# HGRN's transposes and its level of 64 tokens put into the runs of its level products, and HGRN's steps with products held back to follow RWKV's, in a hybrid decoder layer

## The chip, the cores and the metric

The program runs on one core of a Trainium2 chip. The metric is the device time of one execution in microseconds (us). Every comparison is of such times of this kernel before and after the change, on the same inputs.

## What is computed

One decoder layer over 2048 tokens of width 1024, all in float32. An input projection `h @ W_in` feeds two token mixers that run side by side: HGRN2 (4 heads of 128) and RWKV-7 (8 heads of 64). Their outputs are concatenated, projected and added to `x`; a ConvFFN with a depthwise convolution of width 3 follows, and a final RMSNorm. Cut to what matters here:

```
proj = rmsnorm(x, norm1_w) @ w_in
o_hg = HGRN2: S_t = diag(f_t) S_{t-1} + k_t v_t^T,  o_t = S_t^T q_t,  k = 1 - f
o_rw = RWKV-7: S_t = S_{t-1} diag(w_t) + (S_{t-1} a_t) b_t^T + v_t k_t^T,  y_t = S_t r_t
x = x + concat(o_hg, o_rw) @ w_out
x = x + (silu(gate) * val) @ w_down,   gate, val = split(conv3(rmsnorm(x, norm2_w) @ w_up))
out = rmsnorm(x, final_norm_w)
```

## The kernel before

**Two stages.** Stage 1 (`phase1`) does the input projection, both mixers and the output projection of the first three blocks of 512 tokens; stage 2 does the last block's output projection (`wacc`, line 1270) and the ConvFFN. The change touches stage 1 alone.

**Dense products.** A large product is three matmuls of 128 rows by 512 columns, because each operand is split into a high and a low part of type float32r (`mm3`, lines 270 to 272; the weights' split is on lines 254 and 255). Their accumulator in stage 1 is the tile `pj`. They use the whole 128 x 128 array of TensorE (the PE of the profile).

**Small products.** The mixers work with plain float32 products, most of them on a part of the array. In the names of the profile: `rw<-XH,M` and `rw<-AR,XH` (lines 905, 910) are RWKV's eight chunk steps, on 64 x 64 parts; `rw<-TZ,M`, `rw<-TTs,ZT` and `rw<-RHS,TTs` (lines 821, 834, 847) are three links of RWKV's triangular inverse, each of which waits for ScalarE (ACT) to copy the one before out of PSUM (tiles `ZT`, `TTs`, then `UV` and `M`); `rw<-UV,KBT` (line 867) waits for the last of these copies. `hg<-hX` are HGRN's level products: levels of 1 to 16 tokens on line 990 and of 32 tokens on line 997, on 32 columns of the array, and the level of 64 tokens on line 1046, on 64 columns. Whole-array products of HGRN are its transposes (`hg<-ident,hv` line 952, `hg<-ident,hk` line 1044), its state products (`hg<-VT,KT` line 1055) and its output products (`hg<-Af,VT`, `hg<-hq,SH`, lines 1064 and 1065). Sums over a head are float32r products over the whole array (`part,ones` for HGRN, `part,group` for RWKV, in `add_up`, lines 1083 and 1084).

**Order of work.** Three generators are advanced in rounds: RWKV (`rw_stream`, 8 calls of `rw_super`, each for two pairs of heads and 512 tokens), HGRN (`hg_stream`, 16 calls of `hg_unit`, each for one head and 512 tokens) and `dense`. A round is one step of RWKV (up to its next `yield`), one step of HGRN, and then dense work of about 2000 units of cost (`TICK`), which is three groups of three dense matmuls:

```
while any(alive.values()):
    for key, g in (("r", rw_), ("h", hg_)):
        if alive[key]:
            try:
                next(g)
            except StopIteration:
                alive[key] = False
    fill(TICK)
```

The scheduling layer then orders the instructions of each engine from this record, by data, buffers and its own estimates; on the chip each engine runs its list in that order.

**A unit of HGRN** has 15 steps: transpose of `v`; three steps that scale operands on VectorE (DVE) for the levels of 1, 2 and 4 tokens; the products of the diagonal and these levels; three more scalings; the products of the levels of 8, 16 and 32 tokens, which ACT copies into `Af` in six pieces; the scaling of level 64 and of `k` and `q`; the transpose of `k` with the products of level 64, copied by ACT to `KT` and `Af`; the state products; the output products and their square; the sum over the head; the last scaling and the store.

**PSUM.** HGRN has two banks (`bank("hg")`), RWKV two double banks, dense two. A unit takes eight `hg` banks in turn. `hX` has three buffers; the tile `KT` takes the buffer of `Sf`.

Of the kernel before, what the change touches and what calls it, by code (L numbers as in the profile page):

```python
# [18 lines left out]
P = 128  # L19
# [3 lines left out]
BLK = 512  # L23
# [44 lines left out]
def tile_layer(ctx, tc, consts, x, norm1_w, w_in, hg_lb_logits, hg_norm_w, rw_shift_mu, rw_w0, rw_w2,  # L68
# [205 lines left out]
    def phase1(c1):  # L274
# [371 lines left out]

        def rw_super(nb, s_):
# [20 lines left out]
            for u in U:  # L668
                TE.matmul(bs_[u][:, 0, :], w2a2[64:128, pc[u]], tl[64:128, :], start=True, stop=True)
                TE.matmul(bs_[u][:, 1, :], w2a2[0:64, pc[u]], tl[0:64, :], start=True, stop=True)  # L670
# [52 lines left out]
            for j in range(2):  # L723
                for u in U:
                    s1 = bank2()
                    for i in range(4):
                        b, e = 2 * j + i // 2, i % 2
                        for h in range(2):
                            hr = slice(h * 64, h * 64 + 64)
                            TE.matmul(s1[:, h, i * P:i * P + P], KB[hr, 4 * u + b, 2 * e:2 * e + 2, :],  # L730
                                      AR[hr, u, :, 2 * b + e, :], start=True, stop=True)
# [31 lines left out]
            for u in U:  # L763
                for b in range(4):
                    TE.transpose(tp[:, u, b * P:(b + 1) * P], AT[:, u, 2 * b:2 * b + 2, :], ident)
            tpv = tp.rearrange("p u (b h t) -> p (u b) h t", h=2, t=64)
            tq = bank2()
            for u in U:
                for b in range(4):
                    TE.matmul(tq[:, u, b * P:(b + 1) * P], v[:, u, b * P:(b + 1) * P], cen, start=True, stop=True)  # L770
# [9 lines left out]
            for b, h, e, u in quads():  # L780
                kr, c0, sl = 64 - er0(e), col0(u, e), (b * 2 + h) * 64
                TE.matmul(lv[c0:c0 + 64, u, sl:sl + 64], M[kr:kr + 64, e, u, b, h, 0:64],
                          UV[kr:kr + 64, 4 * u + b, e, h * 64:h * 64 + 64], start=True, stop=True,
                          tile_position=(kr, c0))
            lvv = lv.rearrange("p u (b h t) -> p u b h t", h=2, t=64)
# [32 lines left out]
            for b, h, e, u in quads():  # L818
                r0 = er0(e)
                c0, sl = r0 + 32 - 32 * u, u * 256 + (b * 2 + h) * 32  # L820
                TE.matmul(z[c0:c0 + 32, 0, sl:sl + 32], M[r0:r0 + 32, e, u, b, h, 32:64],
# [9 lines left out]
            for b, h, e, u in quads():  # L831
                r0 = er0(e)
                c0, sl = r0 + 32 * u, u * 256 + (b * 2 + h) * 32
                TE.matmul(z2[c0:c0 + 32, 0, sl:sl + 32], ZT[r0 + 32:r0 + 64, u * 8 + b * 2 + h, :],
# [10 lines left out]
            for b, h, e, u in quads():  # L845
                r0, c0, sl = er0(e), col0(u, e), ((b % 2) * 2 + h) * P
                TE.matmul(qus[u][c0:c0 + 64, b // 2, sl:sl + P], TTs[r0:r0 + 64, u * 8 + b * 2 + h, :],
# [15 lines left out]
            for u in U:  # L863
                for ch in range(8):
                    b, e = ch // 2, ch % 2
                    for h in range(2):
                        TE.matmul(xp[h * 64:h * 64 + 64, u, ch * 64:ch * 64 + 64], KBT[:, u, ch, h * 64:h * 64 + 64],
                                  UV[:, 4 * u + b, e, h * 64:h * 64 + 64], start=ch == 0, stop=False,
                                  tile_position=(0, h * 64), skip_group_check=True)
            for u in U:  # L870
                Q, G = M[:, 0, u, :, :, 0:64], M[:, 1, u, :, :, 0:64]
                yg = bank2()
                for w in range(2):
                    for b in range(4):
                        for e in range(2):
                            rs_ = slice(er0(e), er0(e) + 64)
                            sl = w * 256 + b * 64
                            for h in range(2):
                                rhs = (M[rs_, e, u, b, h, 64:128] if w == 0
                                       else KBT[rs_, u, 2 * b + e, h * 64:h * 64 + 64])  # L880
                                TE.matmul(yg[h * 64:h * 64 + 64, e, sl:sl + 64], Q[rs_, b, h, :], rhs,
# [8 lines left out]
            for u in U:  # L890
                for ch in range(8):
                    b, e = ch // 2, ch % 2
                    for h in range(2):
                        c0 = (h ^ u) * 64
                        TE.matmul(yp[c0:c0 + 64, u, ch * 64:ch * 64 + 64],
# [3 lines left out]
            for ch in range(8):  # L899
                b, e = ch // 2, ch % 2  # L900
                cs_ = slice(ch * 64, ch * 64 + 64)
                for u in U:
                    for h in range(2):
                        hr = slice(h * 64, h * 64 + 64)
                        TE.matmul(xp[hr, u, cs_], M[hr, 1, u, b, e, 0:64], XH[hr, u, ch, :], start=False,
                                  stop=ch == 7, tile_position=(h * 64, h * 64), skip_group_check=True)
                for u in U:
                    for h in range(2):
                        hr, c0 = slice(h * 64, h * 64 + 64), (h ^ u) * 64
                        TE.matmul(yp[c0:c0 + 64, u, cs_], XH[hr, u, ch, :], RT[hr, u, ch, :], start=False,  # L910
# [714 lines left out]
```

## Time and profile before

| | us |
|---|---|
| median of 3 runs | 2649.24 |
| lowest and highest run | 2648.57 and 2652.3 |
| the profiled execution | 2645.42 |
| its span, first to last instruction | 2643.6 |
| TensorE busy in that span | 2547.0 |
| VectorE busy | 1963.7 |
| ScalarE busy | 1372.7 |
| GpSimd busy | 382.1 |

All rows of the trace come from the profiled execution, so a row's time is counted from the start of its span. In a row of the timeline the first number is the start and the second the time until the last of the merged instructions ends; consecutive matmuls overlap, so what a matmul costs is read from the starts of its neighbours. A float32 product appears as two matmuls in the trace (x8 there is x4 in the program). `[0.72 <-DVE TZ L808]` says that the engine stood idle for 0.72 us before the row, until that instruction was done.

### The profile page before, as it was taken

The numbers are of one execution on the slowest core, as the hardware profiler recorded it, in microseconds if no ns is written. First come the engines' busy times: TensorE is split into PE (matmuls) and PEld (weight loads), VectorE is DVE, ScalarE is ACT, GpSimd is POOL, SyncE is SP. The second block draws the span as 40 slices with busy tenths as digits, with TensorE's granted clock in tenths as the row PEclk, the third lists the DMA queues.
The fourth block names the chain that finished last, engine by engine and source line by source line (L and its number), as shares of the span: only waits on it lengthen the run. The fifth ranks groups of instructions, "written<-read, shape, count | busy, mean of one in ns | idle before, by whom it ended". The sixth has DMA issues, their size and how long they took to land.

```text
span 2643.6 us, 51054 instructions
## 1 busy us (share of the span) xinstructions
PE 2547.0 (96%) x19467; PEld 2046.8 (77%) x19467; DVE 1963.7 (74%) x3744; ACT 1372.7 (52%) x2258; POOL 382.1 (14%) x686
## 2 busy tenths in 40 slices
PE   7999999999999999899899999999999999999998
PEld 5877777777777767777678888887888887888887
DVE  4868677676576765777678789988988887766556
ACT  5555444555545555344466654556554544545444
POOL 6433222212222122232100000000000000000000
PEclk9999999999999999999999999999999999999999
DMA  8846463555655565845583467747763553998655
GB/s 304 239 147 195 152 168 116 143 159 205 190 173 138 174 212 179 261 151 150 181 287 124 136 221 257 240 154 232 245 203 129 171 171 128 334 321 283 200 191 187
DMA packets 380298, 518.98 MB, mean 196 GB/s; under 512 B 114463, under 2 KB 211093, under 8 KB 380053
## 3 DMA queue, kind: packets, MB, share of 16 engines
q1 hardware_dynamic: 325521, 337.38, 40.1%
q0 software_dynamic: 54464, 178.32, 20.9%
q8 instruction: 153, 2.51, 0.4%
q14 instruction: 92, 0.75, 0.1%
q10 hardware_dynamic: 68, 0.02, 0.0%
HBM read 372.99 MB, written 134.22 MB: 192 GB/s over the span
## 4 chain that ended last, share of the span: by engine, by line
PE 70%; DVE 11%; ACT 8%; DMA 7%; issue 3%; POOL 0%; SPq 0%; DVEq 0%; ACTq 0%; POOLq 0%
PE pj L270 7%; PE pj L271 7%; PE pj L272 6%; PE ua L270 5%; PE ua L272 5%; PE ua L271 5%; PE da L271 3%; PE da L272 3%; PE da L270 3%; PE ud L271 2%; PE ud L270 2%; PE ud L272 2%; PE db L272 2%; PE db L271 2%; PE db L270 2%
## 5 line engine op out<-in xcount | busy, mean ns | idle before, releaser
L270 PE MATMUL pj<-hh,wh 128*128 128x512 f32 x960 | 391.6, 408 | 6.1 <-ACT rkv L122 4.0
L271 PE MATMUL pj<-hl,wh 128*128 128x512 f32 x960 | 377.4, 393 | 0.0
L272 PE MATMUL pj<-hh,wl 128*128 128x512 f32 x960 | 377.4, 393 | 0.0
L270 PE MATMUL ua<-Bh,uwh 128*128 128x512 f32 x704 | 276.4, 393 | 3.5 <-ACT m L122 2.2
L272 PE MATMUL ua<-Bh,uwl 128*128 128x512 f32 x704 | 274.3, 390 | 0.0
L271 PE MATMUL ua<-Bl,uwh 128*128 128x512 f32 x704 | 274.1, 389 | 0.0
L270 PEld LDWEIGHTS pj<-hh,wh 128*128 128x128 f32 x960 | 180.9, 189 | 54.5 <-issue 7.0
L272 PEld LDWEIGHTS pj<-hh,wl 128*128 128x128 f32 x960 | 180.8, 188 | 39.4 <-DMA wl<-Win171l 0.3
L271 PEld LDWEIGHTS pj<-hl,wh 128*128 128x128 f32 x960 | 181.0, 189 | 35.0 <-DVE hl L488 0.5
L254 ACT CAST uwh<-uraw 128x512 fp32r<-128x512 f32 x220 | 134.3, 617 | 135.0 <-PE ua L271 55.7
L255 DVE TENSOR_TENSOR dal<-draw,dah 128x512 fp32r<-128x512 f32 x138 | 95.2, 690 | 108.3 <-ACT dah L254 105.7
L255 DVE TENSOR_TENSOR uwl<-uraw,uwh 128x512 fp32r<-128x512 f32 x220 | 147.1, 684 | 34.3 <-ACT uwh L254 34.3
L254 ACT CAST dah<-draw 128x512 fp32r<-128x512 f32 x138 | 85.8, 621 | 160.0 <-PE da L271 75.5
L270 PEld LDWEIGHTS ua<-Bh,uwh 128*128 128x128 f32 x704 | 132.2, 188 | 33.9 <-ACT m L122 5.6
L272 PEld LDWEIGHTS ua<-Bh,uwl 128*128 128x128 f32 x704 | 132.2, 188 | 28.1 <-DVE uwl L255 0.4
L271 PEld LDWEIGHTS ua<-Bl,uwh 128*128 128x128 f32 x704 | 132.3, 188 | 26.7
L270 PE MATMUL ud<-Bh,uwh 128*128 128x512 f32 x352 | 138.0, 392 | 0.0
L1495 POOL DMA_DIRECT2D gd<-y x2 | 1.1, 542 | 943.1 <-DVE y L1493 943.1
L272 PE MATMUL ud<-Bh,uwl 128*128 128x512 f32 x352 | 137.1, 390 | 0.0
L271 PE MATMUL ud<-Bl,uwh 128*128 128x512 f32 x352 | 137.0, 389 | 0.0
L271 PE MATMUL da<-dbl,dah 128*128 128x512 f32 x332 | 129.4, 390 | 0.2 <-DVE dbl L255 0.2
L272 PE MATMUL da<-dbh,dal 128*128 128x512 f32 x332 | 129.2, 389 | 0.0
(582 smaller groups left out, 6203.0 us busy)
## 6 DMA issues: line engine op xcount, KB each, us to landing
uraw<-in_w_up_dram SPq DMA_DIRECT2D x176, 256.0 KB, 3.2
woraw<-in_w_out_dram POOLq DMA_DIRECT2D x96, 256.0 KB, 3.6
br<-gd SPq DMA_DIRECT2D x88, 256.0 KB, 4.3
draw<-Sg SPq DMA_DIRECT2D x88, 256.0 KB, 3.0
draw<-Tw SPq DMA_DIRECT2D x88, 256.0 KB, 3.9
gd<-y SPq DMA_DIRECT2D x86, 256.0 KB, 3.0
Sg<-br SPq DMA_DIRECT2D x72, 256.0 KB, 2.2
xt<-x1d SPq DMA_DIRECT2D x32, 512.0 KB, 6.5
```

The lines of the kernel that those rows point to most:

```text
L254: S.copy(hi, src)
L255: V.tensor_sub(lo, src, hi.bitcast(F32))
L270: TE.matmul(acc, lh, rh, start=first, stop=False, skip_group_check=skip)
L271: TE.matmul(acc, lh, rl, start=False, stop=False, skip_group_check=skip)
L272: TE.matmul(acc, ll, rh, start=False, stop=last, skip_group_check=skip)
L1495: (dma if end is None else nc.gpsimd.dma_start)(gd_[2 * h + b][fb * P:(fb + 1) * P, :], ys[0][:, b * BLK:(b + 1) * BLK])
```

## The change

`small` wraps every product of the two mixers. It notes the last product of RWKV's step; when a step of HGRN has been chosen to follow it, the first product of that step is given an ordering on TensorE behind it (no wait between engines). A step of HGRN that is marked `"products"` by the `yield` ahead of it is held back for up to two rounds until RWKV's step of the same round issues products; the other steps go as before. In `hg_unit` the transposes of `v` move behind the first level products, level 64 and the transposes of `k` move into the step with the levels of 8 to 32, and level 64 takes the last quarter pair of the bank `l1` (columns 256 to 511) and the buffer `SH` for its operand. A unit then has 13 steps, five of them marked, and takes seven banks. As the rounds are recorded, 80 marked steps occur: 63 of them follow a step of RWKV with products, 16 go alone after two rounds of waiting, and one goes alone because RWKV is over; 52 rounds have no step of HGRN. The number of rounds (386) stays, and so does every instruction, but for ScalarE's table loads: 53 in the order before and 59 after, in the whole program.

```diff
+        turn_ = {"now": None, "r": None, "h": None}
+        def small(f, *args, **kw):
+            i_ = f(*args, **kw)
+            if turn_["now"] == "r":
+                turn_["r"] = i_
+            elif turn_["h"] is not None:
+                tc.add_manual_dep(i_.ins, turn_["h"].ins.name, NOSYNC, reason="one run")
+                turn_["h"] = None
+            return i_
...
-            VT = rp.tile([P, 4, P], F32, tag="VT", name="VT")
-            tp = bank("hg")
-            for b in range(4):
-                TE.transpose(tp[:, b * P:(b + 1) * P], v[:, b * P:(b + 1) * P], ident)
-            act(VT, tp.rearrange("p (b t) -> p b t", t=P), AF.Copy)
-            yield
...
+            def turned(tag, name, src):
+                t_ = rp.tile([P, 4, P], F32, tag=tag, name=name)
+                tp = bank("hg")
+                for b in range(4):
+                    small(TE.transpose, tp[:, b * P:(b + 1) * P], src[:, b * P:(b + 1) * P], ident)
+                act(t_, tp.rearrange("p (b t) -> p b t", t=P), AF.Copy)
+                return t_
...
                 Xs.append(scaled(l))
-                yield
+                yield "products" if l == 2 else None
             l1 = bank("hg")
             level(l1, 192, k, q)
             for l in range(3):
                 level(l1, l * 64, Xs[l], Xs[l], l)
+            VT = turned("VT", "VT", v)
...
+            X = scaled(6)
+            V.tensor_mul(k, k, Sf)
+            V.tensor_mul(q, q, Pf)
+            yield "products"
             l1 = bank("hg")
             for l in range(3, 5):
                 level(l1, (l - 3) * 64, Xs[l - 3], Xs[l - 3], l)
             across(l1, 128, Xs[2])
+            for b in range(4):
+                small(TE.matmul, l1[0:64, 256 + b * 64:320 + b * 64], X[:, b * P:b * P + 64], X[:, b * P + 64:b * P + 128],
+                          start=True, stop=True, tile_position=(0, 0))
+            KT = turned("Sf", "KT", k)
...
+        nxt, held = None, 0
         while any(alive.values()):
+            turn_["r"] = None
+            step("r", rw_)
+            if nxt == "products" and (held < 0 or turn_["r"] is None and alive["r"] and held < 2):
+                held += 1
+            else:
+                turn_["h"] = turn_["r"] if nxt == "products" else None
+                nxt, held = step("h", hg_), 0
+                turn_["h"] = None
             fill(TICK)
```

**How it moves instructions, first place.** TensorE's list at the end of the levels of HGRN's sixth unit. Before, the transposes of `k` and level 64 stood by themselves, behind a chunk step of RWKV, nine dense matmuls after the step before; the levels of 8 to 32 stood further up:

```order
L905 MATMUL rw<-XH,M 64x64 x4
L910 MATMUL rw<-AR,XH 64x64 x4
L1044 MATMUL hg<-ident,hk 128x128 x4
L1046 MATMUL hg<-hX 64x64 x4
L270 MATMUL pj<-hh,wh 128x512
```

After, all levels of the second half stand in one run behind the chunk step, with the transposes last (the product lines all read L651, the line of `small`; `hX_5719` is the operand of level 64):

```order
L651 MATMUL rw<-XH,M 64x64 x4
L651 MATMUL rw<-AR,XH 64x64 x4
L651 MATMUL hg<-hX 32x16 x32
L651 MATMUL hg<-hX 32x32 x8
L651 MATMUL hg<-hX_5719 64x64 x4
L651 MATMUL hg<-ident,hk 128x128 x4
L270 MATMUL pj<-hh,wh 128x512
```

Level 64 has moved up into the run of the other levels, and the transposes now stand at the run's end.

**Second place.** ScalarE's list in the seventh call of `rw_super`, at the three links of the triangular inverse: `ZT` and `TTs` are the copies that the next link waits for, `gdt` and `osq` belong to other work, and `UV` and `M` are the copies that line 867 waits for. Before:

```order
L122 ACTIVATE ZT<-rw 32x256 x4
L122 ACTIVATE TTs<-rw 32x8x32
L122 ACTIVATE gdt<-gdt 128x512
L122 ACTIVATE TTs<-rw 32x8x32 x3
L118 ACT_TABLE_LOAD
L122 ACTIVATE osq<-hg,eps_71 128x512
L122 ACTIVATE osq<-osq 128x512
L122 ACTIVATE UV<-rw 64x4x128 x4
L122 ACTIVATE M<-rw 128x8x64
```

After:

```order
L122 ACTIVATE ZT<-rw 32x256 x4
L122 ACTIVATE KT<-hg 128x512
L122 ACTIVATE TTs<-rw 32x8x32 x2
L122 ACTIVATE Af<-hg 32x4x32 x2
L122 ACTIVATE Af<-A 32x4x32 x4
L122 ACTIVATE Af<-hg 64x4x64
L122 ACTIVATE gdt<-gdt 128x512
L122 ACTIVATE TTs<-rw 32x8x32 x2
L118 ACT_TABLE_LOAD
L122 ACTIVATE UV<-rw 64x4x128 x4
L122 ACTIVATE M<-rw 128x8x64
```

HGRN's copies of its levels (`KT` and seven pieces of `Af`) now stand among the copies of RWKV's chain, half of `TTs` behind them, and the two `osq` steps have left the place ahead of `UV`.

**Third place.** ScalarE's list at the end of stage 1, where the last unit of HGRN ends (`osq`) and stage 2's first operands are made (`woh`, `Bh`). Before:

```order
L122 ACTIVATE yo<-yo 128x1024
L122 ACTIVATE osq<-osq 128x512
L254 CAST wh<-woraw 128x512 x2
L122 ACTIVATE yo<-yo,vt 128x512
L122 ACTIVATE yo<-yo,lnx 64x512 x2
L254 CAST wh<-woraw 128x512
L118 ACT_TABLE_LOAD
L247 CAST woh<-uraw 128x512
```

After:

```order
L122 ACTIVATE yo<-yo,vt 128x512
L122 ACTIVATE yo<-yo,lnx 64x512 x2
L122 ACTIVATE osq<-hg 128x512
L247 CAST part<-osq 128x512
L122 ACTIVATE osq<-hg,eps_71 128x512
L122 ACTIVATE osq<-osq 128x512
L118 ACT_TABLE_LOAD
L247 CAST woh<-uraw 128x512
```

The last unit's square, logarithm and exponential have moved behind RWKV's `yo` to the place directly ahead of the table load. On TensorE the last sum of HGRN (`part,ones`) is now followed by 15 dense matmuls before stage 2's first product, where 33 dense matmuls and RWKV's two gate products (line 936) stood behind it before.

83 lines of the change are left out of this document (36 added, 47 removed).

## Prediction

> **What bounds the kernel now.** I read the page first, then a table of the two stages, then TensorE's timeline, then who waits for whom in stage 1. The page says that TensorE (PE) is the bound: it is busy nearly throughout and most of the chain that ended last is its own.
>
> ```profile
> PE 2547.0 (96%) x19467; PEld 2046.8 (77%) x19467; DVE 1963.7 (74%) x3744; ACT 1372.7 (52%) x2258; POOL 382.1 (14%) x686
> PE 70%; DVE 11%; ACT 8%; DMA 7%; issue 3%; POOL 0%; SPq 0%; DVEq 0%; ACTq 0%; POOLq 0%
> ```
>
> The table of the stretches splits the span at the first product of stage 2 (1312.77); after the two times stand the busy times of PE, its weight loads, DVE, ACT and POOL, then the granted clock.
>
> ```profile
> 0.00:1312.77 1312.77, 1232.64 (x13666) 966.01 (x13666) 907.19 (x2148) 664.94 (x1116) 366.28 (x657) 0.99 0.59 181
> 1312.77:2643.60 1330.83, 1314.40 (x5803) 1080.79 (x5802) 1056.52 (x1597) 707.76 (x1143) 15.86 (x29) 1.00 0.64 211
> ```
>
> All of the change lies in stage 1, where PE stands idle for 1312.77 - 1232.64 = 80.1 us and ACT is busy 51% of the time. Who is waited for there (total, times, longest):
>
> ```profile
> PE vps L156 <- DMA cst<-in_consts_dram: 11.1, 1, 11.1
> PE rw L867 <- ACT M L122: 9.7, 6, 3.6
> PE pj L270 <- ACT hh L247: 6.0, 5, 2.0
> PE hg L1084 <- DVE part L248: 4.4, 7, 1.8
> PE rw L821 <- DVE TZ L808: 3.8, 4, 1.4
> PE hg L1055 <- ACT KT L122: 1.4, 2, 0.8
> ```
>
> The start-up wait (11.1) is not touched. The rest is scattered, and no HGRN wait is large: a gain can come from what small products themselves cost PE, or from RWKV's waits. The first shows in the timeline around a chunk step:
>
> ```profile
> 600.06 0.39 PE L271 MATMUL pj<-wl,hh 128*128 128x512 f32 x1
> 600.28 0.40 PE L272 MATMUL pj<-wh,hl 128*128 128x512 f32 x1
> 600.61 0.39 PE L905 MATMUL rw<-XH,M 64*64 64x64 f32 x6
> ...
> 600.89 0.28 PE L910 MATMUL rw<-AR,XH 64*64 64x64 f32 x6
> 601.10 0.50 PE L270 MATMUL pj<-wh,hh 128*128 128x512 f32 x1
> 601.44 0.39 PE L271 MATMUL pj<-wl,hh 128*128 128x512 f32 x1
> 601.67 0.40 PE L272 MATMUL pj<-wh,hl 128*128 128x512 f32 x1
> ```
>
> Dense starts follow each other by 0.22 to 0.23 us (600.06 to 600.28, 601.44 to 601.67). The first small product starts 0.33 behind the last dense one (0.10 more), and the second dense start behind the run comes 0.34 after the first (0.11 more). A run of products on a part of the array therefore costs 0.21 us beside its products. Whole-array products of HGRN pay nothing of the kind:
>
> ```profile
> 617.92 0.39 PE L272 MATMUL pj<-wh,hl 128*128 128x512 f32 x1
> 618.15 1.05 PE L1055 MATMUL hg<-VT,KT 128*128 128x128 f32 x8
> 618.96 0.48 PE L270 MATMUL pj<-wh,hh 128*128 128x512 f32 x1
> 619.28 0.40 PE L1083 MATMUL rw<-part,group 128*128 128x512 f32 x1
> ```
>
> They start 0.23 behind a dense one; with one matmul lasting about 0.28, (1.05 - 0.28) / 7 = 0.11 apart, eight of them and a dense one (8 x 0.11 + 0.23 = 1.11) fill the 1.13 from 618.15 to 619.28.
>
> **Part by part: the runs.** So three of the moves are worth nothing by themselves: the transposes of `v`, the state products and the output products use the whole array, whether they stand among dense matmuls or behind RWKV. What counts is how many runs on a part of the array there are. Counted in TensorE's two lists they are 195 and 180; runs that hold both RWKV's and HGRN's are 22 and 19. The change thus does not bring HGRN's levels nearer to RWKV than the scheduler had them; the 15 runs fewer come from level 64, which no longer has a run of its own. 15 x 0.21 = 3.1 us less. Bounds: 0, since the same products are issued and only switches go, and 16 x 0.21 = 3.4, one run a unit.
>
> Where level products follow RWKV's, the rows show that the pipeline empties all the same:
>
> ```profile
> 607.50 0.33 PE L910 MATMUL rw<-AR,XH 64*64 64x64 f32 x5
> 607.76 0.72 PE L990 MATMUL hg<-hX 128*32 128x16 f32 x63
> ```
>
> The next tiling starts 0.26 behind the last group, no sooner than a dense matmul behind such a group (600.89 to 601.10, 0.21). The Trainium skill, TensorEngine Tiling (Array Packing), section Key Properties, says that a change of the tiling mode drains TensorE, whatever the mode; this row agrees, and the rule speaks against counting runs. By it one counts changes of mode, 440 before and 416 after; at half of 0.21 each, 24 x 0.10 = 2.4 us would be gained in place of 3.1.
>
> **Table loads.** ACT gets six more, and they and the copies around them have these durations:
>
> ```profile
> 1095.55 0.63 ACT L122 ACTIVATE gdt<-gdt 128x512 f32<-128x512 f32 x1 [0.16 <-DVE gdt L314]
> 1096.19 1.16 ACT L122 ACTIVATE TTs<-rw 32x256 f32<-32x256 f32 x3
> 1097.37 1.28 ACT L118 ACT_TABLE_LOAD   x1
> 1098.66 0.69 ACT L122 ACTIVATE osq<-hg,eps 128x512 f32<-128x512 f32 x1
> 1099.38 0.63 ACT L122 ACTIVATE osq<-osq 128x512 f32<-128x512 f32 x1
> ```
>
> 6 x 1.28 = 7.7 us on an engine that is idle 49% of the stage. It can cost 0 (idle time hides it; a gain is excluded, it is added work) to 7.7 (each load ahead of a copy that PE waits for). Nearest are the two ACT waits above, 9.7 + 6.0 of 1312.77, 1.2% of the stage, which is near the lower end: I take 0.5. The Trainium skill, ScalarE: Activation LUTs, section What ACT_TABLE_LOAD costs, adds a drain of about 1.38 us to a load of 1.28; six would then take 16 us of ACT. The load agrees, the drain doesn't show: the next copy starts 0.01 behind the load's end.
>
> **RWKV's chain.** As the change puts them, level copies fall among the links of the triangular inverse in three of the eight calls (the fifth to seventh). Their price:
>
> ```profile
> 1217.80 0.55 ACT L122 ACTIVATE Af<-hg 32x128 f32<-32x128 f32 x2 [2.41 <-DVE A L1004]
> 1218.36 1.27 ACT L122 ACTIVATE Af<-A 32x128 f32<-32x128 f32 x4
> 1222.88 0.59 ACT L122 ACTIVATE KT<-hg 128x512 f32<-128x512 f32 x1
> 1227.13 0.38 ACT L122 ACTIVATE Af<-hg 64x256 f32<-64x256 f32 x1
> ```
>
> Together 2.8 us. In the seventh call two of the four `TTs` copies stand behind 2.2 of it (without `KT`) and behind `gdt` (0.63): line 847 can start 1.6 + 2.2 + 0.6 = 4.4 us after line 834 (four copies at 1.16 / 3), while TensorE's list has eight dense matmuls and the state products between, 8 x 0.23 + 8 x 0.11 = 2.7. That is a wait of 1.7. In the fifth and sixth the copies stand ahead of `TTs` and start sooner; I put half of that on each, so 3.4 in all. On the other side, the output products (16 matmuls, 1.8 us) now stand between lines 847 and 867 in the same three calls, with nine dense matmuls for 10 to 12: cover for the copies `UV` and `M` grows by about 1.3 us each, and the wait at line 867 is 9.7 / 6 = 1.6 on average, so up to 3.9 less. I take 0 for the two together; bounds -9.7 (all of that wait) and 3 x 2.8 = +8.4.
>
> **End of stage 1.** The last unit of HGRN ends later: 15 dense matmuls follow its last sum, 15 x 0.23 = 3.4 us.
>
> ```profile
> 1302.55 0.50 PE L1084 MATMUL hg<-part,ones 128*128 128x512 f32 x1 [0.22 <-DVE part L248]
> 1312.77 1.16 PE L1270 MATMUL wacc<-woh,Bh 128*128 128x512 f32 x4
> ```
>
> ```profile
> 1311.54 0.62 ACT L247 CAST woh<-uraw 128x512 fp32r<-128x512 f32 x1
> ```
>
> Before there were 10.2 us between. ACT must now do the logarithm, the exponential, a table load and two casts there: 0.69 + 0.63 + 1.28 + 2 x 0.62 = 3.8 us, starting some 0.4 after the sum's start: 4.2 against 0.23 + 3.4. Stage 2's first product waits 0.6, and the sum's operands, queued behind RWKV's `yo` on ACT, perhaps 0.4: +1.0. Below it is 0, if dense work fills in; above it is 10.2 - 3.6 = 6.6, if the store of that head, later by so much, holds its reload on SP's queue and the loads of stage 2 that are queued behind it.
>
> Other edits go together at 0: one PSUM bank fewer, the other buffer of level 64, and the scalings keep their work on DVE. Held steps delay a unit by up to five rounds, but every one of the 386 rounds has dense work before and after, so TensorE's list never runs dry for them; in blocks before the last the stores that go out later are read a block later. Without that cover a held round would cost its HGRN products alone, under 2 us.
>
> **Sum.** -3.1 + 0.5 + 0 + 1.0 = -1.6 us. The profiled execution took 2645.42 (span 2643.6 and 1.8 around it), so 2643.8 for its like; it lies 3.8 under the median of 2649.24, and on the median the sum gives 2647.6. A measurement of this kernel can tell about 0.2%, 5.3 us, from no change: this is no change.
>
> **Rivals.**
> *Waits go too* (faster). For it: line 867's wait is the largest in stage 1 and gets cover; between the transposes of `k` and the state products stand 15 or more dense matmuls in ten units where there were nine, so 1.4 at line 1055 goes, and half of line 1084's 4.4. -3.1 - 3.9 - 1.4 - 2.2 + 1.5 = -9.1: 2640.1. Against it: the waits come where the scheduler's estimates fail, and a new list fails elsewhere.
> *ACT's copies hold RWKV* (slower). The mechanism above with its full price in the three calls and no relief at line 867: -3.1 + 8.4 + 1.5 = +6.8: 2656.0. It decides once the copies between lines 834 and 847 take longer than the 2.7 us of products there. For it speaks the list, which has `Af` ahead of half of `TTs`; against it, that the other five calls have the output products as cover at that place.
> *Every table load is felt* (slower). Six loads of 1.28, each ahead of a copy that PE waits for: -3.1 + 7.7 + 1.0 = +5.6: 2654.8. ACT's idle half speaks against it. The Trainium skill's page on ScalarE, with its drain, would make it twice as much.
> *The change does what its words say.* If all 63 steps that follow RWKV's saved a run, 63 x 0.21 = 13.2 less: 2649.24 - 13.2 + 1.5 = 2637.5. The lists speak against it: 15 runs.
>
> **How the numbers follow.** Forecast 0.48; waits go too 0.28; ACT's copies 0.17; table loads 0.03; the words 0.04. Faster by over 0.2% has 0.28 + 0.04 = 0.32, the same 0.48, slower 0.17 + 0.03 = 0.20. The forecast's own range is 2644 to 2654. To leave out no more than 2 in 10 the range takes in both large rivals' values: 2638 to 2656.
>
> **What would show it.** Right: TensorE's idle time in stage 1 within a few us of 80.1; level 64 starting without the 0.10 of a dense matmul ahead, and the stage about 1 to 3 us shorter. Wrong towards faster: line 867's wait well under 9.7. Wrong towards slower: waits of line 847 on `TTs` of 1.5 us or more in calls five to seven, or stage 2's first product waiting for `woh` by over 1 us. If runs of HGRN alone cost much more or less than 0.21, the first term is wrong.

## The result, and the profile after

The changed kernel takes 2672.18 us (median of 4 runs, 2669.62 to 2676.13), the kernel before, run beside it, 2648.9 (4 runs, 2648.4 to 2652.3). The ratio is 1.0086, 95% interval 1.0071 to 1.0102: slower by 0.86%, 23 us, where no change was forecast and 2656 was the upper end of the range. The profiled execution took 2669.62 us, with a span of 2667.8. These are the page's rows for it:

```profile
PE 2554.8 (96%) x19467; PEld 2061.5 (77%) x19467; DVE 1966.9 (74%) x3744; ACT 1381.9 (52%) x2264; POOL 381.9 (14%) x686
PE 58%; issue 16%; DVE 9%; DMA 7%; ACT 6%; POOL 4%; SPq 0%; POOLq 0%; DVEq 0%; ACTq 0%
```

The table of the stretches, split where stage 2's first product starts (columns as before):

```profile
0.00:1333.75 1333.75, 1239.15 (x13665) 979.31 (x13665) 910.87 (x2149) 673.54 (x1122) 366.92 (x659) 0.97 0.59 178
1333.75:2667.80 1334.05, 1315.66 (x5802) 1082.16 (x5802) 1056.04 (x1596) 708.39 (x1143) 14.96 (x28) 1.00 0.64 211
```

Stage 1 is 21.0 us longer, stage 2 is 3.2 us longer. In stage 1 TensorE stands idle for 94.6 us (80.1 before) and is busy 6.5 us longer with the same products. The granted clock of the stage fell from 0.99 to 0.97. Over the whole span it is, in the view of the cores, first before:

```profile
core 0: 2643.6 us, clock 0.994
```

```profile
core 0: 2667.8 us, clock 0.983
```

The clock knows two values here, 1 and 0.5, so a mean of 0.983 is 2 x 0.017 x 2667.8 = 91 us at half speed, and 0.994 is 32 us. The trace's record of the clock has 81.9 and 27.3 of these in stage 1 (after the start-up), in 11 dips and 6. Half speed shows in the timeline of the changed kernel: dense starts, 0.23 us apart before, are 0.43 apart:

```profile
1297.62 0.63 PE L270 MATMUL pj<-wh,hh 128*128 128x512 f32 x1
1298.05 0.63 PE L272 MATMUL pj<-wh,hl 128*128 128x512 f32 x1
1298.48 0.63 PE L271 MATMUL pj<-wl,hh 128*128 128x512 f32 x1
```

Who is waited for in stage 1 (in the changed kernel all small products stand on line 651, so the waits go by the tile that releases them: `TZ` is old line 821's, `ACT M` old line 867's):

```profile
PE pj L270 <- ACT hh L247: 11.2, 7, 3.0
PE rw L651 <- DVE TZ L821: 8.3, 5, 2.2
PE rw L651 <- DVE AR L900: 7.7, 7, 2.7
PE hg L651 <- issue: 4.0, 3, 2.9
PE rw L651 <- DVE M L897: 3.9, 4, 1.8
PE pj L443 <- ACT xt L122: 3.7, 4, 1.7
PE rw L651 <- ACT M L122: 1.8, 5, 1.1
PE rw L651 <- ACT TTs L122: 0.4, 1, 0.4
```

The largest wait of before (9.7, line 867) is nearly gone, as the prediction had it; `hh`, `TZ` and `AR` (6.0, 3.8 and 4.3 before) have grown by 13.1 together. What a wait costs now is seen around the first one on `TZ`:

```profile
134.97 0.39 PE L272 MATMUL pj<-hh,wl 128*128 128x512 f32 x1
137.51 0.75 PE L651 MATMUL rw<-TZ,M 32*32 32x32 f32 x64 [2.15 <-DVE TZ L821]
...
142.98 0.80 PE L651 MATMUL hg<-Af,VT 128*128 128x128 f32 x2
```

```profile
135.00:138.40 3.40, 1.25 (x67) 0.85 (x66) 3.19 (x9) 2.86 (x5) 2.73 (x5) 1.00 0.44 159
138.40:148.60 10.20, 10.20 (x126) 8.69 (x129) 6.26 (x17) 4.12 (x10) 2.76 (x5) 0.50 0.57 183
148.60:152.00 3.40, 3.40 (x47) 2.80 (x40) 0.44 (x2) 2.32 (x4) 0.00 (x0) 1.00 0.00 0
```

TensorE is idle for 2.15 us, is busy for 1.25 of a slice of 3.4 us, and the clock is 0.50 for the next 10.2 us, in which it has work throughout. Before, the same place looked so: HGRN's output products and its sum stood ahead of the product of `TZ`, with no wait on `TZ` there.

```profile
130.97 0.38 PE L1064 MATMUL hg<-Af,VT 128*128 128x128 f32 x2
...
136.57 0.50 PE L1084 MATMUL hg<-part,ones 128*128 128x512 f32 x1 [0.87 <-DVE part L248]
...
138.52 0.75 PE L821 MATMUL rw<-TZ,M 32*32 32x32 f32 x64
```

In the changed kernel the output products are held until RWKV has products again, and stand behind them (142.98). Before, they had been part of the work that covers RWKV's solve on VectorE.

### The profile page after: what moved, and what is told of

Read it like the earlier page. It is cut to its first block, busy times and chain, and to the rows that moved or that the text cites. A ratio compares the mean times of both kernels' runs of the same rounds, so it can differ in the third digit from the quotient of the medians.

```text
span 2667.8 us, 51031 instructions
## 1 busy us (share of the span) xinstructions
PE 2554.8 (96%) x19467; PEld 2061.5 (77%) x19467; DVE 1966.9 (74%) x3744; ACT 1381.9 (52%) x2264; POOL 381.9 (14%) x686
## 4 chain that ended last, share of the span: by engine, by line
PE 58%; issue 16%; DVE 9%; DMA 7%; ACT 6%; POOL 4%; SPq 0%; POOLq 0%; DVEq 0%; ACTq 0%
PE ua L270 5%; PE ua L272 5%; PE ua L271 5%; PE pj L270 4%; PE pj L271 4%; PE pj L272 4%; PE rw L651 3%; PE da L271 3%; PE da L272 3%; PE da L270 3%; PE ud L271 3%; PE ud L270 3%; PE ud L272 3%; PE db L271 2%; PE db L272 2%
```

## The experiments

Three things had to be told apart: which part of the change makes the waits, whether the half clock follows from waits, and what the stops marked "issue" are. In this table each has its own ratio to the kernel before; stage 1, TensorE's idle time and time at half clock in it (the start-up left out), and its stops (waits for "issue", which are part of the idle time) are of one profile each, worked out from the trace. A profiled execution is not the median one: that of hold_only took 2648.11 us, 8.6 under its median. In the kernels with products of no use at their start these fill 3.3 to 6.6 us of the start-up wait, so their idle time is to be compared among themselves.

| run | median us | ratio (95%) | stage 1 | idle | half clock | stops |
|---|---|---|---|---|---|---|
| before | 2648.9 | 1 | 1312.8 | 80.1 | 27.3 | 4.8 |
| changed kernel | 2672.18 | 1.0086 (1.0071 to 1.0102) | 1333.8 | 94.6 | 81.9 | 8.0 |
| merge_only | 2666.16 | 1.0064 (1.0039 to 1.0089) | 1331.0 | 86.2 | 51.2 | 9.3 |
| order_only | 2670.99 | 1.0078 (1.005 to 1.0107) | 1338.6 | 92.3 | 58.0 | 13.6 |
| hold_only | 2656.66 | 1.0032 (1.0015 to 1.0049) | 1315.2 | 85.5 | 44.4 | 10.3 |
| hold_and_order | 2665.91 | 1.0064 (1.004 to 1.0087) | 1327.9 | 88.4 | 68.3 | 5.5 |
| held_fill | 2671.71 | 1.0084 (1.0067 to 1.01) | 1338.0 | 98.1 | 75.1 | 21.3 |
| hold_fill | 2661.26 | 1.0053 (1.0034 to 1.0073) | 1322.1 | 82.7 | 51.2 | 10.2 |
| merge_split | 2663.44 | 1.0054 (1.0037 to 1.007) | 1329.4 | 86.1 | 44.4 | 8.7 |
| before_again | 2647.54 (one run) | | 1316.4 | 79.3 | 41.0 | 5.5 |
| before_shift | 2652.07 | 1.0005 (0.9994 to 1.0015) | 1319.2 | 76.4 | 41.0 | 4.5 |
| before_half | 2648.58 | 1.0003 (0.9991 to 1.0015) | 1315.2 | 70.9 | 54.6 | 1.5 |
| merge_shift | 2665.99 | 1.0064 (1.0046 to 1.0081) | 1334.5 | 81.9 | 51.2 | 8.1 |
| merge_half | 2659.04 | 1.0031 (1.0018 to 1.0045) | 1321.2 | 80.9 | 30.7 | 8.3 |
| after_shift | 2670.61 | 1.0074 (1.0049 to 1.0099) | 1334.7 | 93.1 | 75.1 | 12.1 |
| after_half | 2658.47 | 1.0031 (1.0016 to 1.0046) | 1323.3 | 84.4 | 75.1 | 6.2 |
| late_steps | 2651.03 | 1.0012 (1.0001 to 1.0023) | 1314.7 | 84.9 | 51.2 | 2.1 |
| late_unmerged | 2650.82 | 1.0 (0.9987 to 1.0012) | 1315.9 | 83.7 | 47.8 | 3.7 |

### The parts of the change

**Merged steps alone.** In the changed kernel:

```diff
-            if nxt == "products" and (held < 0 or turn_["r"] is None and alive["r"] and held < 2):
+            if False:
...
-                turn_["h"] = turn_["r"] if nxt == "products" else None
+                turn_["h"] = None
```

> The changed kernel's HGRN unit in 13 steps (level 64 and the transposes inside the runs of the level products), but no step is held back and no product is ordered behind RWKV's: every round takes one step of each, as before. Three theories of the 23 us. Cover: holding HGRN's steps takes their products out of the rounds in which RWKV solves on VectorE, so TensorE reaches RWKV's and the dense products before their inputs are ready; its waits grow long, and each long wait is followed by slices of 3.4 us at half clock. By it this kernel is near the kernel before: 2645 to 2652 us, granted clock 0.991 or more, under 10 half-clock slices in stage 1. Merged steps: the longer steps queue more copies on ScalarE at once (four Af copies, KT, the level 64 copy) ahead of the dense copies hh; by it this kernel keeps most of the loss: 2662 to 2675 us, clock near 0.984. Order: the loss comes from HGRN's products standing behind RWKV's; by it this kernel is near the kernel before, as by Cover.

**Holding, without the order** (the steps stay merged): only the second of these two edits.

> The changed kernel with its marked steps held back up to two rounds, but without the order between HGRN's first product and RWKV's last one. Cover: the loss stays, 2660 to 2678 us, granted clock 0.987 or less, 15 or more half-clock slices in stage 1, TensorE waits on TZ, AR and hh as in the changed kernel. Order: the loss goes, 2645 to 2653 us, clock 0.992 or more. Merged steps: the loss stays as by Cover (the run of merged steps alone tells these two apart).

**The order, without holding** (the steps stay merged): only the first of them.

> The changed kernel with nothing held back: each round takes one step of each stream, and where both have products in it, HGRN's stand behind RWKV's. Cover: near the kernel before, 2644 to 2653 us, granted clock 0.991 or more. Order: most of the loss, 2660 to 2675 us. Merged steps: most of the loss, 2660 to 2675 us.

**Holding and order on the unit of 15 steps:** `hg_unit` as before, with its products in `small` and six of its `yield`s marked `"products"`.

> The kernel before's HGRN unit in 15 steps (level 64 and the transposes in steps of their own), its six steps with products after the first held back and ordered behind RWKV's as in the changed kernel. Cover: the loss is there without the merged steps, 2660 to 2685 us, granted clock 0.987 or less. Merged steps: near the kernel before, 2645 to 2654 us, clock 0.992 or more. Order: the loss is there, as by Cover (the runs of holding alone and of the order alone tell these two apart).

Measured: 2666, 2657, 2671 and 2666. No theory has all four. Cover failed on merged steps alone and on the order alone, which should have been free; Merged steps failed on the unit of 15 steps; Order failed on merged steps alone. And 2657, of merged steps that are held, lies between the ranges of all three, so all three missed it. Merging costs 17 us by itself, and holding with the order costs as much without merging. But the parts don't add up: merging and order cost 22 us, holding on top of both leaves it at 23, and holding on top of merging alone takes some 9 of the 17 away again. What holds of Cover is the part on `TZ`: its wait is 7.8, 9.2 and 8.3 us in the three kernels that hold, 3.0 and 2.3 in those that don't, and 3.8 before. The wait on `hh` is 9.8 with holding and order on the unit of 15 steps and 11.2 in the changed kernel, 4.8 and less in the other three.

### Does the half clock follow from the waits?

**Pauses.** In the kernel before, every eighth step of the down product in stage 2:

```diff
+                    if i == 0 and (s_ - DS) % 8 == 6 and WAITS:
+                        for w_ in range(WAITS.pop(0)):
+                            p_ = nc.gpsimd.memset(pd, 0.0)
+                            if w_ == 0:
+                                tc.add_manual_dep(p_.ins, last_.ins.name, SYNC, reason="pause")
...
+                        tc.add_manual_dep(first_.ins, pause_[0].ins.name, SYNC, reason="pause")
```

> The kernel before, with 16 pauses of TensorE put into its last stage, 8 steps of the down product apart: a dense product waits for 1 to 8 fills of a scratch tile on GpSimd, which start when the product ahead of it ends (about 0.6 us each; 1 to 8, then 1 to 8 again, 43 us in all). Theory Clock: a pause that empties about half of a 3.4 us slice is followed by at least one slice at half clock, so pauses under about 1.5 us cost what they last and those over about 2 us cost at least 1.7 us more; 10 or more dips of the clock after the 10 pauses of 4 fills or more, none after the 4 shortest, and a time of 2649 + 43 + 17 to 35, or 2709 to 2730 us. Rival (the clock falls by some other rule, and waits and dips only stand beside each other): no dips at the pauses, and 2685 to 2697 us.

It took 2660.07 us, below both forecasts, and tells nothing of the clock: the scheduler put later products ahead of the waiting one, and one pause of 16 was felt by more than 0.7 us. In the second try the next 48 dense products all wait:

> The pauses again, now so that TensorE can't take later products ahead of them (in the first try it ran up to 14 dense products in the meantime, and 15 of 16 pauses were hidden): the next 48 dense products all wait for the fills of the scratch tile. 16 pauses of 1 to 8 fills of 0.53 us, twice, 38 us of fills in all. Theory Clock: a pause that leaves TensorE busy for under half of one 3.4 us slice is followed by 3.4 us or more at half clock: all pauses of 6 to 8 fills (3.2 to 4.2 us), some of those of 3 to 5, depending on where in the slice they fall, none of those of 1 or 2; 8 to 12 dips, each costing 1.7 us or more beside the pause: 2649 + 38 + 14 to 25, or 2700 to 2713 us. Rival (dips and waits only stand beside each other): at most one dip at the pauses, and 2685 to 2692 us.

It took 2724.12 us (2 runs), over the range of both theories. One pause of four fills, in the timeline, and the granted clock of its slice and the two behind it:

```profile
2360.75 0.39 PE L273 MATMUL da<-dbh,dal 128*128 128x512 f32 x1
2363.59 0.50 PE L271 MATMUL da<-dbh,dah 128*128 128x512 f32 x1 [2.45 <-POOL pd L1582]
2363.93 0.40 PE L272 MATMUL da<-dbl,dah 128*128 128x512 f32 x1
...
2364.71 0.63 PE L272 MATMUL da<-dbl,dah 128*128 128x512 f32 x1
```

```profile
2361.06:2364.47 3.41, 0.96 (x5) 0.73 (x5) 1.36 (x2) 1.24 (x2) 2.10 (x4) 1.00 1.03 398
2364.47:2367.88 3.41, 3.41 (x10) 2.63 (x9) 0.57 (x1) 1.14 (x2) 0.00 (x0) 0.51 0.46 170
2367.88:2371.29 3.41, 3.41 (x17) 2.78 (x16) 1.25 (x3) 1.14 (x2) 0.00 (x0) 0.99 0.49 154
```

Eight of the 16 pauses were followed by 3.4 or 6.8 us at half clock: all seven that emptied 0.72 or more of one slice, and one of the nine others, which emptied 0.55 or less (one of five that emptied 0.53 to 0.55). The same 2.45 us, put by chance across a border of two slices (0.53 of one), cost nothing more. The pauses are 51 us; stage 2 has 47 us at half clock for 7 before, so 0.5 x 40 = 20; together 71 of the 75 measured. So a wait does cause the half clock: the dips are at the pauses, as Clock had it, though its range ended 11 us too low because two pauses ran longer than their fills (5.3 and 8.6 us).

The same count over stage 1 of 20 profiles (all kernels here), in slices of 3.413 us on the grid of the clock's record: when TensorE was busy for under 0.4 of a slice at full clock, the next one was at half in 80 of 80; from 0.4 to 0.5, 64 of 76; from 0.5 to 0.6, 25 of 95; from 0.6 to 0.8, 22 of 456; above, 1 of 6576. Of the 192 dips in these 20 profiles of stage 1, 188 last one to three slices (3.4 to 10.2 us), one four and three five. The Trainium skill, TensorE: Matmul & The Clock Gate, Part 1, has a free-running window of 3413 ns and half clock after an idle window; the length agrees, but no idle window is needed: about 2 us idle in one is enough in most cases.

### Cover and supply

**More dense work in held rounds.**

```diff
                 held += 1
+                fill(TICK + 1200)
...
-            fill(TICK)
+                fill(TICK - 190)
```

> The changed kernel with its dense work shared out unevenly: 3200 ns of it in a round whose HGRN step is held back, 1810 in every other one (2000 in all rounds before). Theory Cover: the waits on TZ come from rounds that holding has emptied, so this gives them their work back: waits on TZ under 5 us (8.3 in the changed kernel), fewer than 8 dips of the clock, 2645 to 2660 us. Rival (the waits come from the order and from HGRN's work standing together on VectorE and ScalarE): the waits on hh, AR and M stay, 2664 to 2678 us.

**Dense work between RWKV's products and HGRN's**, on merged steps alone:

```diff
+            if turn_["r"] is not None and nxt == "products":
+                fill(TICK / 2)
+                nxt = step("h", hg_)
+                fill(TICK / 2)
```

> The kernel with merged steps alone, but where both streams have products in a round, half of the round's dense work (1000 ns) stands between RWKV's products and HGRN's. Theory Supply: where 150 or more small products follow each other within 3 us, TensorE outruns the fetch of its instructions (blocks of 16 KB) and stands still for 1 to 3 us in the middle of a row of products that wait for nothing; those waits are 8.5 us in the run of merged steps alone, and dense products in between take them away: under 3 us, fewer dips of the clock, 2648 to 2660 us in spite of some 40 more changes between small and dense products. Rival (the loss of merged steps comes from later copies and splits): waits for instructions may go, but the time stays at 2660 to 2675 us.

**The kernel before once more:**

> The kernel before, once more, unchanged: how far waits and clock differ from one profile to the next. If the order sets them, the long waits stand at the same places, with 4 to 9 dips of the clock in stage 1 and 20 to 45 us at half clock; if chance does, another list of waits, and dips anywhere.

The waits of held_fill, as the trace lists them:

```profile
PE hg L651 <- issue: 14.9, 5, 4.7
PE pj L270 <- ACT hh L247: 10.2, 7, 3.0
PE rw L651 <- DVE M L897: 6.3, 5, 2.3
PE rw L651 <- issue: 4.5, 2, 2.7
PE rw L651 <- DVE TZ L821: 3.6, 3, 2.0
```

`TZ` fell from 8.3 to 3.6 and `AR` from 7.7 to 2.4, as Cover had it, but the stops rose to 21.3, the dips were 12 (11 in the changed kernel) and the time stayed at 2671.71, where the rival had it. Splitting (2663.44, in the rival's range) left the stops at 8.7, so that remedy of Supply failed: stops still come in HGRN's own run of products. The repeat of before gave the same waits (8.6 on `M`, 8.0 on `hh`, 4.3 on `AR`) and 41 us at half clock for 27: the waits are of the order, the dips in part of chance. A stop, in merged steps alone:

```profile
935.62 0.79 PE L651 MATMUL hg<-hX 128*32 128x16 f32 x68
939.22 0.43 PE L651 MATMUL hg<-hX 128*32 128x16 f32 x27 [2.81 <-issue]
```

The row of level products breaks off for 2.81 us though none of them waits for a semaphore. The DMA packets of the queue for TensorE's instructions are 153 blocks of 16 KB in the whole program (for 19467 matmuls and their weight loads, so about 127 matmuls to a block; that it is 128 the shifts below bear out), and one ran here from 936.99 to 937.96; the products went on 1.26 us later. In the 20 profiles there are 90 such stops of over 0.3 us in stage 1 behind small products, and 89 end 1.20 to 1.75 us after such a block has landed (median 1.38). The median stop has 122 small matmuls in the 3 us ahead of it, where dense ones would be 13. The column of stops in the table also holds those among dense matmuls (22 of over 0.3 us in the 20 profiles), which this count leaves out.

**Moving the blocks.** At the start of the program, ahead of the first transpose, 64 products of no use, and then 32:

```diff
+        for _ in range(64):
+            TE.matmul(vps[0:32, 0:32], ident[:, 0:32], ident[:, 0:32], start=True, stop=True)
         TE.transpose(vps[:, :P], rows, ident)
```

> The kernel before with 64 small products of no use at its very start, where TensorE waits for the first loads; nothing else is changed, and the order of the rest is the same. They move the borders of the 16 KB blocks in which TensorE's instructions are fetched (128 products with their weight loads in a block) by half a block. Theory Supply: where a run of small products meets a border, TensorE stands until about 1.4 us after the next block's fetch has ended; the places of these stops move with the borders, and the kernel before has few of them (4.0 and 5.5 us in its two profiles) by its phase: after the shift they stand at other places, 3 to 15 us, and the time lies between 2646 and 2665 us. Rival (those stops have to do with the products and their data, not with the fetch): the stops stay at the same products, and the time is the same within 0.2%.

> The kernel with merged steps alone (2666 us, 9.3 us of stops for no visible reason, five of them among HGRN's level products at 56, 37, 18, 2 and 73 places past a border), with the same 64 small products at its start. Theory Supply: the stops leave those level products, since the borders now fall 64 products earlier or later, under 5 us of them or at other products; the time falls by 3 to 10 us, to 2655 to 2664. Rival: stops at the same products, 2662 to 2670 us.

> The changed kernel with the same 64 small products at its start. Its stops for instructions were 7.3 us, in five places. Theory Supply: they move; between 3 and 15 us, and the time stays within 2662 to 2682 us, since the waits on hh, TZ, AR and M, 35 us, are not touched. It is a second profile of the changed kernel as well: those waits should stand at the same products, with 60 us or more at half clock. Rival (the changed kernel lost by its phase alone): stops under 4 us and 2648 to 2660 us.

These expectations rested on a slip: a float32 product is two matmuls, so 64 products are 128 of them, one whole block, and every border stayed at the same product. The stops came at the same products, and the times were those of the kernels without the shift, as both theories would have it. Half a block tells them apart:

> The kernel before with 32 fp32 products of no use at its very start, which are 64 records: half a block of instructions (the 64 products of the first try were 128 records, one whole block, and its stops came at the same products). Theory Supply: the stops (4.0, 5.5 and 4.5 us in the three profiles of this order, around records 11242, 11365, 11747 and 13521) leave those products and come at others, half a block away, 2 to 15 us; time 2645 to 2665 us. Rival (the stops belong to the products and not to the borders): the same products, 64 records later, and 2646 to 2654 us.

> The changed kernel with the same half block at its start. Theory Supply: the stops (7.3 and 12.1 us in two profiles of this order, around records 7575, 9222, 11124, 11756 and 13404) leave those products; 2 to 20 us of stops at others. The time stays between 2655 and 2680 us, since the waits on hh, TZ, AR and M are of the order and stay, with 60 us or more at half clock. Rival (the stops belong to the products): the same five places, and 2666 to 2675 us.

> The kernel with merged steps alone, with half a block of instructions of no use at its start. Theory Supply: its 17 us hang on the borders that fall into the level products; shifted by half a block, the stops of 9.3 and 8.1 us fall under 5 us and the time to 2648 to 2660 us. Rival (the merged steps cost by what they do to the copies and splits, whatever the borders): stops may move, but 2661 to 2670 us.

The stops stay at a place in the stream of instructions and leave the products. Counted along TensorE's list, the changed kernel stops at matmul 11124, with a whole block ahead at 11252, the same product, and with half a block ahead at 11125, which is 63 matmuls earlier in the work. In the same way merged steps alone stop at matmul 6181 with half a block ahead and without. None of the kernel before's five products is stopped at after its half block, where 1.5 us of stops are left. And the changed kernel gained 12 us with no other edit: ratio 1.0031, where the whole block gave 1.0074. Its other waits are those of the changed kernel (its lines stand two lower):

```profile
PE pj L272 <- ACT hh L249: 11.8, 7, 3.2
PE rw L653 <- DVE TZ L823: 8.8, 5, 2.3
PE rw L653 <- DVE AR L902: 7.5, 7, 2.8
PE hg L653 <- issue: 4.4, 2, 3.9
```

Between the two shifts stops went from 12.1 to 6.2 us. But against the changed kernel without a shift (8.0) they fell by 1.8 alone, while stage 1 fell by 10.4. So the half block did make this kernel faster, and fewer stops are shown to be a part of the reason only. Merged steps alone gained 7 us, but not by fewer stops (8.1 and 8.3): they fell elsewhere, and 51.2 us at half clock became 30.7. So Supply's count failed there, though its time was met and the shift of the borders again changed it. The Trainium skill, Runtime: NRT & Kernel Launch, Instruction fetch mechanics, has the blocks of 16 KiB and calls the crossing of a border mostly hidden; among small products it isn't, by these 89 stops.

### Which steps, and what to keep

**Only the three later steps held and ordered:** in the changed kernel the `yield`s ahead of the two steps of level products lose their mark.

> The changed kernel, but its two steps of level products are neither held nor ordered; only the three later steps with products (the sums of state, the outputs, the norm: 48 steps instead of 80) are. Theory Runs (the loss hangs on the level products, whose 128 or more records in a row stand behind RWKV's and whose copies then come late): waits on hh under 7 us, stops under 6, fewer than 9 dips, 2648 to 2660 us. Rival (merging and holding of any steps cost the same): 2662 to 2675 us.

**Holding alone, with its dense work given back:** held_fill without the order.

> The kernel that only holds (2656.7 us), with 3200 ns of dense work in a round whose HGRN step is held and 1810 in every other. Theory Cover: the waits on TZ and AR (17 us there) fall to under 9, as they did with the same filling in the changed kernel (16 to 6); with the stops for instructions at 4 to 10 us the time is 2638 to 2652 us. Rival (filling the held rounds thins out the others, and the stops and the waits on hh and M grow, as they did in the changed kernel, where stops went from 7 to 21 us): 2656 to 2672 us.

**The three later steps held and ordered, on the unit of 15 steps:**

> The kernel before's HGRN unit in 15 steps, with the holding and the order of the changed kernel for its three last steps with products alone (sums of state, outputs, norm). Theory Light steps: few products (4 to 16 calls a step) join RWKV's runs, so TensorE changes less often between small and dense products (253 runs of small products for 279) and no long run of records is made; about 0.3 us a run gives 8 us, the waits on AR, TZ and hh take 0 to 8 of them back: 2638 to 2650 us. Rival (any step moved out of its round costs cover): waits on AR, TZ and hh grow by more than 8 us, and 2650 to 2665 us.

late_steps took 2651.03 us. It differs from the changed kernel only in that the two steps of level products (with the transposes in them) are neither held nor ordered, and that is 0.74% of the 0.86. Its waits:

```profile
PE rw L651 <- DVE AR L900: 12.2, 6, 5.9
PE pj L270 <- ACT hh L247: 11.6, 11, 2.3
PE rw L651 <- DVE TZ L821: 7.2, 5, 2.1
```

Theory Runs had its time and its stops right (2.1 us) but not its wait on `hh`, which stayed, nor its dips (10). The three waits shown are 31.0 us together, more than the 27.2 of the changed kernel, so they are not what tells the two apart. What is smaller is the stops, by 5.9 of the 9.7 us of idle time, and the half clock, 51.2 us for 81.9. The same kind of wait can be followed by a long dip or a short one. This one, in the changed kernel, by 10.2 us at half clock:

```profile
286.85 0.75 PE L651 MATMUL rw<-TZ,M 32*32 32x32 f32 x64 [1.76 <-DVE TZ L821]
```

And this one, in late_steps, by 3.4:

```profile
281.40 0.75 PE L651 MATMUL rw<-TZ,M 32*32 32x32 f32 x64 [1.68 <-DVE TZ L821]
```

What sets the length of a dip is not shown here. hold_fill (2661.26) went the way of the rival: `TZ` and `AR` fell from 17.2 to 8.2 as forecast, a wait on `M` grew from 0.5 to 6.9 us in their stead. late_unmerged (2650.82, ratio 1.0) neither gains nor loses, at the lower end of the rival's range: 26 fewer runs of small products, and 20.4 us of waits on `AR` and `TZ` for 8.1. No version here beats the kernel before.

## Why the prediction was wrong

**The runs.** Taken at -3.1. The busy time rose by 6.5, but 81.9 - 27.3 = 54.6 us more passed at half clock, of which TensorE worked through 47; at starts 0.427 us apart for 0.227 that cost 22, so the work at full clock shrank by about 15, an estimate. In TensorE's lists the runs of small products between dense ones fell from 279 to 225, which the prediction did not count, since a row had shown that whole-array products pay nothing for their place. The sign was right and the size too small. The same estimate gives 1216.8 to 1221.7 us of work in six profiles of before's order and 1205.8 to 1206.9 in three of the changed one's, 14 less in the mean (products of no use left out). That fewer runs are the reason is argued only, and merged steps alone speak against it: with 249 runs, 30 fewer than before, they have 1221.7 us of work. The six other kernels that hold steps have 1209.8 to 1217.0, the five that merge and hold none 1219.9 to 1223.3, so the gain goes with holding.

**RWKV's chain.** Taken at 0, from -3.9 on the cover of line 867 and +3.4 on `TTs`. The first came larger (9.7 to 1.8), the second not at all (0.5 to 0.4), so the rival of ScalarE's copies did not come about. Had this been all, the change would have been faster.

**Table loads.** Taken at 0.5. There are six more in the stage (44 to 50), and TensorE's waits (of over 0.15 us, the start-up left out) that fall together with loads went from 7.6 to 8.7 us. So the loads can have cost 1.1 at most, and the term was about right. merge_only has 54 loads and 8.2 us of such time.

**End of stage 1.** Taken at +1.0. Stage 2's operand is waited for, for 0.5 us where 0.6 was taken, and the sum's for 1.3 where 0.4 was; the term is 0.8 short:

```profile
PE hg L651 <- ACT part L247: 1.3, 1, 1.3
PE wacc L1291 <- ACT Bh L247: 0.5, 1, 0.5
```

**The step that failed** is the one that put the held steps at 0: "every one of the 386 rounds has dense work before and after, so TensorE's list never runs dry for them", with "under 2 us" as the price of a held round. With the marks taken off the two steps of level products (late_steps) 20 of the 23 us go, so holding and ordering these steps, with the rest of the change in place, cost 20 us and not 0. The list does not run dry, but a held step's products are missing ahead of the next product that waits for VectorE: the wait on `TZ` grew from 3.8 to 8.3 us, and three of the 11 dips of the changed kernel, 30.7 of its 81.9 us at half clock, stand right behind such a wait. The profile of before had the evidence: line 821 waited at four of its eight places, 3.8 us in all, with HGRN's products ahead of it, so it had little slack to lose. The rivals priced ScalarE's copies in RWKV's chain and not VectorE's solve. Missing cover is not the whole of the 20 us, though: late_steps has these waits too, and costs almost nothing.

**The term that was missing** is the clock. Every sum took it as constant, while the table of the stretches said 0.99 and not 1. A wait of 2 us in one slice costs 2 us and then about half of 3.4 to 10.2. Idle time is 14.5 us up, the half clock costs about 22 more and the work is about 15 down, which is the 21 us of stage 1; the sum closes by the way the work was worked out, so it is a division of the loss and no check of it. Stage 2 is 3.2 longer, and one dip of 3.4 us that it didn't have explains 1.7 of it.

What stays open: how the 20 us of the held level products divide between missing cover, stops and the chance of where a wait falls; and how much of the changed kernel's 23 us is the place of its block borders (after_half says about 12, one shift of one size). Why merged steps alone cost 17 us but, with the later steps held, almost nothing is open as well. The two have the same time at half clock (51.2 us) and nearly the same idle time (86.2 and 84.9); by the estimate above, 12 of the 16 us between their profiles are work at full clock (1221.7 and 1209.8).

## What to carry to other kernels

When work is moved out of a round, look at which wait stood behind it and how much slack that wait had; a list that never runs dry is no cover by itself. Price a wait of TensorE by where it falls: several short ones cost their length, one that empties more than half of a 3.4 us slice mostly costs 1.7 to 5 us more here. In runs of a hundred and more small products count instruction blocks too, and try a shift by half a block before an order is judged, since it was worth 0.4% here.

## What the runs showed of the hardware

In stage 1, half clock mostly follows a slice of 3.413 us in which TensorE was busy for under 0.5 (144 of 156 slices), hardly ever one with over 0.6 (23 of 7032); it lasts one to three slices in 188 of 192 dips. Instructions for TensorE come in 153 blocks of 16 KB, a block in about 1 us (0.97 in the one above), and 89 of 90 stops behind small products end 1.20 to 1.75 us after one has landed; such stops lasted up to 4.7 us. Neither shows as a wait on an engine: the first lengthens busy time, the second stands as "issue".
